# Latents ahead of the context between two layers, and three heads summed in PSUM at the end

## The chip, the cores and the metric

The kernel runs on one NeuronCore of a Trainium2 chip. The metric is the device time of one execution in microseconds (us). Before the change the median of three runs was 1581.88 us (1580.87 to 1582.18).

## What is computed

A two-layer backbone on 512 latent tokens and 256 context tokens of width 1024, all in fp32. Cut to what matters here:

```python
for i in range(2):
    shift, scale, gate = split(silu(c) @ ada_w[i] + ada_b[i])        # and the same from c_ctx
    h  = rms(x,   norm_g[i]) * (1 + scale)   + shift                 # latents
    hc = rms(ctx, norm_g[i]) * (1 + scale_c) + shift_c               # context
    yc, y = hgrn2_mixer(hc, h, ...) if i == 0 else rglru_mixer(hc, h, ...)
    x = x + gate * y
    if i == 0:
        ctx = ctx + gate_c * yc
return rms(x, final_norm_g)
```

Layer 0 (HGRN2) has 16 heads, each with four input projections, a recurrence and an output projection `w_out`. Layer 1 (RG-LRU) has 8 heads of 256 channels. Each takes `h @ w_in` (a branch `xb` for latents and context, a gate branch `g` for latents alone), a convolution over four tokens, sigmoid gates `r` and `i` by two 256x256 products in two directions, `a = exp(-8 r softplus)`, `u = sqrt(1 - a^2) * i * xb`, a linear scan in both directions, `(forward + backward) * silu(g)`, and an output product with its 256 rows of `w_out`. Layer 1 needs the context only to start its latent scans.

## The kernel before, in words

All tensors lie with channels on the 128 partitions and the 768 tokens (context in columns 0 to 255, latents in 256 to 767) along the free axis. The residual stream `x1` is 8 tiles of 128 channels. A product in fp32 precision is made of three float32r matmuls (`mm3`, L307): high times high, high times low, low times high. So every weight, loaded as 512 KB of raw fp32 by the SP queue, is split by ScalarE (`hi`, L129) and VectorE (`lo`, L130). The split weights have three buffers each (`hip`, `lop`), the raw ones three (`rawp`); `W.slots` lets named weights use other buffers. `Weights.get` takes the weights in the order in which the program asks for them, loads three ahead, and splits the next one early while `presplit` is set.

PSUM has eight banks, four in the pool `dps` (`dtile`) and four in `aps` (`atile`). The tile framework orders each engine's instructions from the program's order, its own estimate of what is ready, and priorities (`high_priority(n)` lifts an instruction by n places); each engine then runs its list strictly in order. `issue_after` keeps ScalarE's table sets together.

**Between the layers.** The program runs head 15's recurrence (L720) with the sum of the outputs of heads 12 to 14 as filler. A block of the adaLN product (`ada_block`, L224: 16 matmuls in fp32 on raw weights, a copy, 4 small matmuls) is woven into each of heads 9 to 14 by `extra` (L707); the last block of layer 1, number 5, goes into head 14. Then come: the output of head 15 (`out_item` with `accs`, L391), first for the 256 context tokens, all eight channel tiles, then for the 512 latents. After each tile VectorE adds gate times PSUM to `x1` (L405), ScalarE squares it (L285, L288) and GpSimd (tiles 1 to 3) or VectorE (tiles 5, 6) adds the square to one of three accumulators (L289). `norm1` makes the reciprocal root mean square of each segment: matmuls against a column of ones (L262), a square root (L265), a reciprocal (L266), a broadcast by matmuls (L272). Then `hchunk` (L296) normalizes one channel tile (VectorE L300, ScalarE L304, VectorE L305), and the first products of layer 1, into four `dtile` banks and one `atile` bank, follow tile by tile: first all context tiles (`rc`, two banks), then all latent tiles (`rl`, three banks; L739 to L743). `conv` (L776) evacuates them with a priority of 400. `rin(0, ALL[1:2])` (L895) is the product that follows.

**Layer 1.** For each head j a `mixer` (L817) first makes the gates: for each of four keys (direction, channel half) four PSUM tiles and sigmoids (L840). Then follow tanh and two exponentials per key (L849 to L852), square roots (L858), and the scans (L863 to L867), with the sum, the silu gate and the split of y (`yh` L872, `yl` L873). `phase` weaves other products in between: those of the next head (`rin`) and the output of the head before (`rout`, L881), whose eight PSUM tiles VectorE adds to `x1` (L879). R, Gt and T have four buffers each, y two. Heads 0 to 5 take `rin` of the next head whole. Head 6 takes only its `xb` part with its gates, and `rout(5)` behind them. The last head takes its own `g` part while three of its four keys' gates are made, and the fourth key as a group of its own. Then come `rout(6)`, the last head's output for its first channel half (`part(d, (0,), ...)`), where tiles 5 to 7 are added at once and tiles 0 to 4 stay in PSUM, and for its second half in two column halves, each with adds, squares, sums and the final norm (L937 to L956).

## Time and profile before

| | us |
|---|---|
| median of 3 runs | 1581.88 |
| the profiled execution, its own time | 1581.96 |
| its span, first to last instruction | 1580.2 |
| TensorE busy in the span | 1531.5 |
| VectorE, ScalarE, GpSimd busy | 1207.8, 902.6, 12.7 |

The mean granted TensorE clock is 0.985 of full speed. Times in the trace count from the start of the span. In a row of the timeline the first figure is the start, the second the length; in brackets stands how long the engine had been idle before, and what ended it. A matmul's length includes its way through the array, so a run of them is counted from start to start. L is a line of the kernel. Layer 0 ends, and layer 1 starts, around 1075 to 1133 us; the last head of layer 1 begins at about 1502.

### The profile page before, as it was taken

Reading aid. Unit: us, or ns where it says so; the run is one execution under the profiler, and the core shown is the slowest. Engines: PE = TensorE matmul, PEld = TensorE weight load, DVE = VectorE, ACT = ScalarE, POOL = GpSimd, SP = SyncE. Lnnn points to the kernel's source line nnn. Section 1 sums busy time; section 2 is a strip of 40 time slices with the busy share of each in tenths; the row PEclk is TensorE's granted clock in tenths of the full one; section 3 lists DMA queues with packets and bytes.
Section 4 is the critical chain, followed back from the end, with each engine's and each line's share of the span. In section 5 each row is a group of like instructions: output and inputs, shape, how many; then the busy total and the mean of one; then the engine's idle time right before and its main releaser. Section 6 shows DMA issues by size and latency. Waiting matters only on the chain.

```text
span 1580.2 us, 34022 instructions
## 1 busy us (share of the span) xinstructions
PE 1531.5 (97%) x14740; PEld 1431.9 (91%) x14740; DVE 1207.8 (76%) x1867; ACT 902.6 (57%) x1423; POOL 12.7 (1%) x16
## 2 busy tenths in 40 slices
PE   5999999999999999999999999998999999999995
PEld 3899999999999999999999999987889988988984
DVE  4767678768867868867876786787768887797888
ACT  4554555555554554554545555654577577667874
POOL 0000000000000000000000000001000000000001
PEclk8999999999999999999999999998999999999996
DMA  8231311110211211223232132202212213222111
GB/s 324 84 121 55 95 55 41 55 55 28 82 41 42 68 41 55 81 68 95 68 95 82 55 108 68 95 15 67 67 54 81 83 51 94 80 77 70 55 53 54
DMA packets 33861, 116.80 MB, mean 74 GB/s; under 512 B 3632, under 2 KB 6064, under 8 KB 33712
## 3 DMA queue, kind: packets, MB, share of 16 engines
q1 hardware_dynamic: 32192, 113.26, 23.0%
q8 instruction: 116, 1.90, 0.5%
q10 hardware_dynamic: 1520, 1.37, 0.3%
q14 instruction: 33, 0.27, 0.1%
HBM read 112.52 MB, written 2.10 MB: 73 GB/s over the span
## 4 chain that ended last, share of the span: by engine, by line
PE 93%; DVE 3%; ACT 2%; issue 1%; POOL 1%; DMA 0%; POOLq 0%; ACTq 0%; DVEq 0%
PE in L311 12%; PE in L312 11%; PE in L313 11%; PE v L381 9%; PE lv L460 4%; PE r L313 4%; PE r L312 4%; PE r L311 4%; PE o L565 4%; PE gt L311 3%; PE gt L312 3%; PE gt L313 3%; PE o L311 3%; PE o L313 3%; PE o L312 3%; PE U L533 2%
## 5 line engine op out<-in xcount | busy, mean ns | idle before, releaser
L311 PE MATMUL in<-h_hi,hi 128*128 128x384 f32 x1024 | 350.6, 343 | 3.4 <-ACT h_hi L304 2.7
L312 PE MATMUL in<-h_lo,hi 128*128 128x384 f32 x1024 | 345.8, 338 | 0.3 <-DVE h_lo L305 0.3
L313 PE MATMUL in<-h_hi,lo 128*128 128x384 f32 x1024 | 344.9, 337 | 0.0
L130 DVE TENSOR_TENSOR lo<-raw,hi 128x1024 fp32r<-128x1024 f32 x160 | 195.2, 1220 | 88.1 <-ACT hi L129 84.7
L129 ACT ACTIVATE hi<-raw 128x1024 fp32r<-128x1024 f32 x160 | 168.2, 1057 | 121.3 <-PE in L312 48.7
L311 PEld LDWEIGHTS in<-h_hi,hi 128*128 128x128 f32 x1024 | 193.1, 189 | 16.8 <-issue 9.9
L312 PEld LDWEIGHTS in<-h_lo,hi 128*128 128x128 f32 x1024 | 193.1, 189 | 2.8 <-issue 1.6
L313 PEld LDWEIGHTS in<-h_hi,lo 128*128 128x128 f32 x1024 | 192.8, 189 | 1.2 <-issue 0.8
L509 DVE TENSOR_TENSOR QQ<-QQ,T 128x768 f32<-128x768 f32 x112 | 117.8, 1052 | 20.8 <-ACT qt L491 20.5
L416 ACT ACTIVATE kt<-KK 128x768 f32<-128x768 f32 x112 | 102.4, 915 | 41.1 <-DVE KK L502 32.7
L502 DVE TENSOR_TENSOR KK<-KK,T 128x768 f32<-128x768 f32 x112 | 117.6, 1050 | 9.7 <-ACT kt L416 8.2
L313 PE MATMUL r<-h_hi,lo 128*128 128x512 f32 (+1 forms) x344 | 123.4, 359 | 0.3 <-DVE lo L130 0.3
L312 PE MATMUL r<-h_lo,hi 128*128 128x512 f32 (+1 forms) x344 | 123.1, 358 | 0.0
L311 PE MATMUL r<-h_hi,hi 128*128 128x512 f32 (+1 forms) x344 | 122.9, 357 | 0.0
L337 ACT ACTIVATE sg<-in 128x384 f32<-128x384 f32 x128 | 61.5, 482 | 99.9 <-PE in L313 99.7
L381 PE MATMUL v<-hi,h_hi 128*128 128x256 f32 x384 | 111.3, 290 | 0.0
L381 PE MATMUL v<-hi,h_lo 128*128 128x256 f32 x384 | 107.4, 280 | 0.0
L381 PE MATMUL v<-lo,h_hi 128*128 128x256 f32 x384 | 107.3, 279 | 0.0
L588 DVE RECIPROCAL sq<-sq 128x384 f32<-128x384 f32 x30 | 76.3, 2545 | 21.1 <-ACT sq L582 20.9
L405 DVE SCALAR_TENSOR_TENSOR x<-o,ada,x 128x256 f32<-128x256 f32 (+1 forms) x184 | 82.3, 488 | 11.3 <-PE o L313 10.6
L311 PE MATMUL o<-rhi,hi 128*128 128x384 f32 (+2 forms) x240 | 85.0, 356 | 1.5 <-DVE lo L130 1.2
L313 PE MATMUL gt<-xh,lo 128*128 128x384 f32 x256 | 86.0, 336 | 0.0
(207 smaller groups left out, 3284.4 us busy)
## 6 DMA issues: line engine op xcount, KB each, us to landing
raw<-in_hgw_dram SPq DMA_DIRECT2D x64, 512.0 KB, 3.7
raw<-in_ada_dram SPq DMA_DIRECT2D x48, 512.0 KB, 4.2
raw<-in_rgi_dram SPq DMA_DIRECT2D x32, 512.0 KB, 3.6
raw<-in_hgv_dram SPq DMA_DIRECT2D x16, 512.0 KB, 3.6
raw<-in_hgo_dram SPq DMA_DIRECT2D x16, 512.0 KB, 3.6
raw<-in_rgg_dram SPq DMA_DIRECT2D x16, 512.0 KB, 3.6
raw<-in_rgo_dram SPq DMA_DIRECT2D x16, 512.0 KB, 3.6
x<-in_x_dram SPq DMA_DIRECT2D x8, 384.0 KB, 5.9
```

What stands on the lines that cost most here:

```text
L129: self.nc.scalar.activation(hi, r, AF.Copy)
L130: self.nc.vector.tensor_tensor(lo, r, hi.bitcast(F32), ALU.subtract)
L311: PE.matmul(ps, lhsT=wh, rhs=xh, start=first and i == 0, stop=False, skip_group_check=skip)
L312: PE.matmul(ps, lhsT=wh, rhs=xl, start=False, stop=False, skip_group_check=skip)
L313: PE.matmul(ps, lhsT=wl, rhs=xh, start=False, stop=last and i == n - 1, skip_group_check=skip)
L381: PE.matmul(ps, lhsT=xh[:, kk, t], rhs=w[:, k], start=part == 0 and k == 0 and i == 0 and c % 2 == 0, stop=part == 1 and k == 3 and i == 2 ...
L405: V.scalar_tensor_tensor(xs, ps[:, a - c.start:b - c.start], gate[:, d, 1 - j:2 - j], xs, ALU.mult, ALU.add)
L416: A.activation(view(kt, 0, [[2 * B, n], [B, 2], [1, B]]), view(KK, 0, [[2 * B, n], [NT + B, 2], [1, B]]), AF.Copy)
L460: PE.matmul(ps[w * g:w * g + w, w * c:w * c + w], lhsT=kt[:, o:o + w], rhs=rhs, start=c == 0, stop=c == NC - 1, skip_group_check=True, til ...
L502: V.tensor_tensor(kv, kv, view(T, 1, [[2, n], [m - 1, 2], [0, B]]), ALU.mult)
L509: V.tensor_tensor(qv, qv, view(T, m + 1, [[2, n], [-m - 1, 2], [0, B]]), ALU.mult)
L588: V.reciprocal(rs, rs)
```

## The change

Between the layers the adaLN block 5 moves from head 14 to the place behind the latents of head 15's output; the latents' output, norm, chunks and first products go ahead of those of the context, the context's output tiles stand one by one behind the latents' chunks, and its norm and products come last. Block 5's raw weights and the split weight of the first `g` product get wide buffers of layer 0. `conv` of head 0 has no priority any more. At the end, head 6 takes the rest of `rin(7)`; the outputs of heads 5, 6 and 7 are summed in the eight PSUM banks (`held`) and added to `x1` once; the last head's four keys are one group; and the final tiles go in the order 4 to 7, 0 to 3, with the groups of the sum of squares to match.

```diff
--- before.py
+++ after.py
@@ -288,7 +288,7 @@
             A.activation(t, x1[:, k, c], AF.Square)
             (nc.gpsimd if i == 0 and len(groups) == 3 else V).tensor_tensor(accs[i][:, c], accs[i][:, c], t, ALU.add)
 
-    THREE = ((0, 1, 2, 3), (4, 5, 6), (7,))
+    THREE, LAST = ((0, 1, 2, 3), (4, 5, 6), (7,)), ((4, 5, 6, 7), (0, 1, 2), (3,))
 
     segs = (slice(0, CTX), slice(CTX, NT))
     lat = segs[1]
@@ -388,14 +388,12 @@
                         A.activation(st[2 * g + u]["V"][:, 2 * b:2 * b + 2], src[:, :, P * u:P * u + P], AF.Copy)
                 yield 1300.0
 
-    def out_item(heads, accs=None, done=None):
+    def out_item(heads):
         ws = [wget("out", h) for h in heads]
         gate = ada[0][:, 2]
-        parts = segs if accs else halves
-        order = [(d, i) for d in range(DK) for i in range(2)]
-        for d, i in sorted(order, key=lambda x: x[1]) if accs else order:
+        for d, i in [(d, i) for d in range(DK) for i in range(2)]:
             e = slice(P * d, P * d + P)
-            c = parts[i]
+            c = halves[i]
             ps = dtile(f"o{heads[0]}_{d}_{i}")[:, :c.stop - c.start]
             mm3(ps, [(w[0][:, e], w[1][:, e], st[h]["r"][0][:, c], st[h]["r"][1][:, c]) for h, w in zip(heads, ws)])
             for j, g in enumerate(segs):
@@ -404,10 +402,6 @@
                     xs = x1[:, d, a:b]
                     V.scalar_tensor_tensor(xs, ps[:, a - c.start:b - c.start], gate[:, d, 1 - j:2 - j], xs,
                                            ALU.mult, ALU.add)
-            if accs:
-                sumsq(accs, THREE, lambda n: ktp.tile([P, NT], F32, name=n, tag="kt"), d, c)
-                if d == DK - 1:
-                    done(i)
             yield 490.0 * len(heads)
 
     def gather(KK, kt, B):
@@ -611,6 +605,9 @@
     for i in range(16):
         W.slots["ada", 0, i // 4, i % 4] = (rawp, "raw", 1024) if i in (10, 11) else wide[(i if i < 10 else i - 2) % 6]
     W.slots["v", 0, 0] = (wide[2], wide[0])
+    for j in range(4):
+        W.slots["ada", 1, 5, j] = wide[(0, 1, 5, 1)[j]]
+    W.slots["rin", 0, 1, 0] = (wide[0], wide[1])
 
 
     acc0 = kdp.tile([P, NT], F32, name="acc0", tag="kd")
@@ -707,7 +704,7 @@
     def extra(h):
         if h in (1, 2):
             return [ada_block(0, 3 + h)]
-        return [ada_block(1, h - 10)] if h >= 10 else []
+        return [ada_block(1, h - 10)] if 10 <= h < NH - 1 else []
 
     for h in range(NH):
         if h == 0:
@@ -721,26 +718,46 @@
         run_all(side)
     accs1 = [pl.tile([P, n], F32, name=f"acc1_{i}", tag=t)[:, :NT]
              for i, (pl, t, n) in enumerate(((kdp, "kd", NT), (qp, "q", NT), (sp, "S", 2 * (NC - 1) * P)))]
-    rs1 = []
-
-    def norm1(i):
+    rs1 = {}
+
+    def norm1(i, between=()):
         c = segs[i]
-        rs1.extend(rstd_of([chunks(a, c) for a in accs1], ones_d, f"h1_{i}", ((c.stop - c.start) // P,)))
-
-    run_all(out_item((NH - 1,), accs1, norm1))
+        rs1[i], = rstd_of([chunks(a, c) for a in accs1], ones_d, f"h1_{i}", ((c.stop - c.start) // P,), between)
+
+
+
+    w15 = wget("out", NH - 1)
+
+    def out_last(d, i):
+        e, c = slice(P * d, P * d + P), segs[i]
+        ps = dtile(f"o{NH - 1}_{d}_{i}")[:, :c.stop - c.start]
+        mm3(ps, [(w15[0][:, e], w15[1][:, e], st[NH - 1]["r"][0][:, c], st[NH - 1]["r"][1][:, c])])
+        V.scalar_tensor_tensor(x1[:, d, c], ps, ada[0][:, 2, d, 1 - i:2 - i], x1[:, d, c], ALU.mult, ALU.add)
+        sumsq(accs1, THREE, lambda n: ktp.tile([P, NT], F32, name=n, tag="kt"), d, c)
+
+    for d in range(DK):
+        out_last(d, 1)
+    side = ada_block(1, 5)
+    for _ in range(4):
+        next(side)
+    norm1(1, side)
 
 
     W.presplit = False
     wx = [wget("rin", 0, 0, e) for e in range(2)]
-    first = [[(w, dtile(f"rc{e}")[:, :CTX]) for e, w in enumerate(wx)]]
     wg = wget("rin", 0, 1, 0)
-    first.append([(w, (dtile if e < 2 else atile)(f"rl{e}")) for e, w in enumerate(wx + [wg])])
-    scr = [ktp.tile([P, NT], F32, name=f"scr1_{k}", tag="kt") for k in range(2)]
-    for i, c in enumerate(segs):
+    first = {1: [(w, (dtile if e < 2 else atile)(f"rl{e}")) for e, w in enumerate(wx + [wg])]}
+    for i in (1, 0):
+        c = segs[i]
         for k in range(DK):
-            hchunk(1, k, i, rs1[i], scr[k % 2])
+            hchunk(1, k, i, rs1[i], ktp.tile([P, NT], F32, name=f"scr1_{i}_{k}", tag="kt"))
             for w, ps in first[i]:
                 mm3(ps, hpairs(w, c, [k]), first=k == 0, last=k == DK - 1)
+            if i:
+                out_last(k, 0)
+        if i:
+            norm1(0)
+            first[0] = [(w, dtile(f"rc{e}")[:, :CTX]) for e, w in enumerate(wx)]
     W.presplit = True
     l0.close()
 
@@ -773,7 +790,7 @@
             turn["gsig"] = A.activation(s["gs"][:, e], ps, AF.Sigmoid)
         V.tensor_tensor(s["gs"][:, e], ps, s["gs"][:, e], ALU.mult)
 
-    def conv(j, e, i, ps):
+    def conv(j, e, i, ps, last=1):
 
         s = rt[j]
         if "xb" not in s:
@@ -785,12 +802,13 @@
         n = segs[i].stop - segs[i].start
         cw = prm_("conv_w").rearrange("p (c t) -> p c t", t=4)[:, 2 * j + e]
         urgent = ExitStack()
-        urgent.enter_context(tc.high_priority(400))
+        if j:
+            urgent.enter_context(tc.high_priority(400))
         A.activation(y, ps, AF.Identity, scale=cw[:, 2:3], bias=prm_("conv_b", 2 * j + e, 1))
         for tap, sh in ((1, 1), (0, 2), (3, -1)):
             src, dst = (ps[:, :n - sh], y[:, sh:]) if sh > 0 else (ps[:, 1:], y[:, :n - 1])
             V.scalar_tensor_tensor(dst, src, cw[:, tap:tap + 1], dst, ALU.mult, ALU.add)
-        if i == 1:
+        if i == last:
             A.activation(s["xh"][:, e], xb, AF.Copy)
             V.tensor_tensor(s["xl"][:, e], xb, s["xh"][:, e].bitcast(F32), ALU.subtract)
         urgent.close()
@@ -818,8 +836,6 @@
 
 
         s = rt[j]
-        yh = s["yh"] = yp.tile([P, 2, LAT], F32R, name=f"yh{j}", tag="yh")
-        yl = s["yl"] = yp.tile([P, 2, LAT], F32R, name=f"yl{j}", tag="yl")
         comb, parts = {}, {}
         for keys in groups:
             for d, jc in keys:
@@ -841,6 +857,9 @@
                     yield 1.0
                 V.tensor_tensor(Gt, Gt, s["xb"][:, jc], ALU.mult)
             yield None
+            if "yh" not in s:
+                s["yh"], s["yl"] = [yp.tile([P, 2, LAT], F32R, name=f"{t}{j}", tag=t) for t in ("yh", "yl")]
+            yh, yl = s["yh"], s["yl"]
 
             for d, jc in keys:
                 R, Gt, T = comb[d, jc]
@@ -888,43 +907,47 @@
             add_out(ps, d, early)
             yield 1300.0
 
-    for i in range(2):
+    for i in (1, 0):
         for e in range(2):
-            conv(0, e, i, first[i][e][1])
+            conv(0, e, i, first[i][e][1], 0)
     g_evac(0, 0, first[1][2][1])
     run_all(rin(0, ALL[1:2]))
+    def part(ws, j, d, us, c):
+        e = slice(P * d, P * d + P)
+        return [(ws[u][0][:, e], ws[u][1][:, e], rt[j]["yh"][:, u, c], rt[j]["yl"][:, u, c]) for u in us]
+
+
+    pss = []
+
+    def held(j, ds, ws):
+        ws.extend([] if ws else [wget("rout", 2 * j + e) for e in range(2)])
+        for d in ds:
+            if len(pss) == d:
+                pss.append((dtile if d < 4 else atile)(f"ro{d}"))
+            mm3(pss[d], part(ws, j, d, (0, 1), slice(0, LAT)), first=j == RH - 3, last=False, skip=True)
+            yield 1300.0
+
     for j in range(RH):
-        last = j == RH - 1
-        m = mixer(j, (((0, 0), (1, 0), (0, 1)), ((1, 1),)) if last else (((0, 0), (1, 0), (0, 1), (1, 1)),))
+        m = mixer(j, (((0, 0), (1, 0), (0, 1), (1, 1)),))
         if j < RH - 2:
             phase(m, 8.0, rin(j + 1, ALL[:2]), 10400.0)
             phase(m, 20.0, chain_([rin(j + 1, ALL[2:])] + ([rout(j - 1)] if j else [])), 26000.0 if j else 15600.0)
-        elif not last:
+        elif j < RH - 1:
             phase(m, 8.0, rin(j + 1, ALL[2:]), 5000.0)
-            phase(m, 20.0, rout(j - 1), 10400.0)
+            for _ in range(4):
+                next(m)
+            phase(m, 12.0, rin(j + 1, ALL[:2]), 5200.0)
         else:
-            phase(m, 6.0, rin(j, ALL[:2]), 10400.0)
-            run_all(m)
-
-
-    run_all(rout(RH - 2, 0))
-    j = RH - 1
-    s = rt[j]
+            w5 = []
+            phase(m, 8.0, held(j - 2, range(4), w5), 5200.0)
+            run_all(held(j - 2, range(4, DK), w5))
+            phase(m, 20.0, held(j - 1, range(DK), []), 10400.0)
+
+
     accs2 = [cp.tile([P, NT], F32, name=f"acc2{i}", tag="R") for i in range(3)]
     ws = [wget("rout", 2 * j + e) for e in range(2)]
-
-    def part(d, us, c):
-        e = slice(P * d, P * d + P)
-        return [(ws[u][0][:, e], ws[u][1][:, e], s["yh"][:, u, c], s["yl"][:, u, c]) for u in us]
-
-    pss = []
     for d in range(DK):
-        ps = (dtile if d < 4 else atile)(f"ro{j}_{d}")
-        mm3(ps, part(d, (0,), slice(0, LAT)), last=d >= 5, skip=True)
-        if d < 5:
-            pss.append(ps)
-        else:
-            add_out(ps, d, 0)
+        mm3(pss[d], part(ws, j, d, (0,), slice(0, LAT)), first=False, last=False, skip=True)
     H, rsf = LAT // 2, []
     fin = [[pl.tile([P, 2, NT], F32, name=f"fin{i}_{t}", tag=t)[:].rearrange("p u n -> p (u n)")[:, :4 * H]
             .rearrange("p (k n) -> p k n", k=4) for pl, t in o] for i, o in
@@ -937,12 +960,12 @@
     for i in range(2):
         c = slice(H * i, H * i + H)
         cx = slice(CTX + H * i, CTX + H * i + H)
-        for d in range(DK):
-            ps = pss[d][:, c] if d < 5 else (dtile if i else atile)(f"ro{j}_{d}_{i}")[:, :H]
-            mm3(ps, part(d, (1,), c), first=d >= 5, last=d >= 5 or i == 1, skip=True)
+        for n, d in enumerate((4, 5, 6, 7, 0, 1, 2, 3)):
+            ps = pss[d][:, c]
+            mm3(ps, part(ws, j, d, (1,), c), first=False, last=i == 1, skip=True)
             add_out(ps, d, 0, cx)
-            sumsq(accs2, THREE, lambda n: cp.tile([P, NT], F32, name=n, tag="G"), d, cx)
-            if i == 1 and d == 4:
+            sumsq(accs2, LAST, lambda n: cp.tile([P, NT], F32, name=n, tag="G"), d, cx)
+            if i == 1 and n == 4:
                 stats(0)
     stats(1)
     for i, rs in enumerate(rsf):
```

## Rows read from the trace of the kernel before

**Rows 1.** The page: TensorE's busy time, and the chain that ended last.

```profile
PE 1531.5 (97%) x14740; PEld 1431.9 (91%) x14740; DVE 1207.8 (76%) x1867; ACT 902.6 (57%) x1423; POOL 12.7 (1%) x16
...
PE 93%; DVE 3%; ACT 2%; issue 1%; POOL 1%; DMA 0%; POOLq 0%; ACTq 0%; DVEq 0%
```

**Rows 2.** Busy time by stretch; columns: PE, PEld, DVE, ACT, POOL, clock, DMA share, GB/s.

```profile
1030.00:1045.00 15.00, 11.92 (x287) 10.23 (x287) 14.95 (x24) 8.59 (x12) 0.00 (x0) 1.00 0.11 37
1075.40:1078.20 2.80, 0.81 (x5) 0.41 (x3) 2.70 (x4) 2.80 (x5) 0.00 (x0) 0.95 0.21 25
1078.20:1081.60 3.40, 3.35 (x15) 3.15 (x16) 3.40 (x6) 1.59 (x4) 0.47 (x1) 0.54 0.79 280
...
1091.40:1094.80 3.40, 0.11 (x2) 0.02 (x1) 3.30 (x4) 2.51 (x4) 3.25 (x2) 1.00 0.07 11
1094.80:1105.30 10.50, 10.50 (x50) 10.50 (x51) 6.97 (x15) 3.17 (x7) 0.00 (x0) 0.51 0.29 96
...
1075.40:1133.40 58.00, 50.24 (x243) 42.45 (x242) 47.12 (x78) 31.87 (x53) 7.75 (x6) 0.88 0.21 64
```

**Rows 3.** TensorE's timeline between the layers.

```profile
1075.25 0.34 PE L313 MATMUL o<-r,lo 128*128 128x384 f32 x1
...
1094.78 1.68 PE L262 MATMUL msh<-cst,acc 128*128 128x1 f32 x8 [3.29 <-POOL acc L289]
...
1128.47 0.40 PE L311 MATMUL r<-h_hi,hi 128*128 128x512 f32 x1
...
1133.14 0.40 PE L313 MATMUL r<-h_hi,lo 128*128 128x512 f32 x1
```

**Rows 4.** GpSimd's timeline between the layers.

```profile
1089.80 4.92 POOL L289 TENSOR_TENSOR acc<-acc,sq 128x512 f32<-128x512 f32 x3 [5.53 <-ACT sq L288]
```

**Rows 5.** VectorE's timeline between the layers.

```profile
1109.73 1.41 DVE L300 SCALAR_TENSOR_TENSOR scr<-x,amul,rbh 128x512 f32<-128x512 f32 x2
1111.98 2.50 DVE L792 SCALAR_TENSOR_TENSOR xb<-rc,prm,xb 128x255 f32<-128x255 f32 x6 [0.85 <-ACT xb L789]
```

**Rows 6.** TensorE by line and form, whole span: all twelve adaLN blocks.

```profile
L230 PE MATMUL ada<-raw,sc 128*32 128x256 f32 x384 | 32.5, 412 | 14.0 <-DMA raw<-in_ada_dram 14.0
...
L240 PE MATMUL adat<-cst,blk 128*128 128x2 f32 x96 | 11.5, 241 | 0.7 <-ACT blk L236 0.7
```

**Rows 7.** Busy time by stretch, as rows 2, last head.

```profile
1541.00:1548.20 7.20, 0.00 (x0) 0.00 (x0) 7.20 (x8) 5.80 (x9) 0.00 (x0) 0.82 0.00 0
1548.20:1555.80 7.60, 7.27 (x15) 4.91 (x16) 7.46 (x11) 2.90 (x3) 0.00 (x0) 0.50 0.00 0
```

**Rows 8.** TensorE's timeline at the end.

```profile
1548.20 2.09 PE L311 MATMUL ro<-yh,hi 128*128 128x512 f32 x3 [7.53 <-ACT yh L872]
...
1557.91 0.99 PE L311 MATMUL ro<-yh,hi 128*128 128x256 f32 x7
```

**Rows 9.** VectorE by line, 1485 to 1580 us: busy, mean ns, idle before.

```profile
L879 DVE SCALAR_TENSOR_TENSOR x<-ro,ada,x 128x512 f32<-128x512 f32 (+1 forms) x35 | 20.6, 623 | 2.7 <-PE ro L313 2.7
...
L861 DVE TENSOR_TENSOR G<-G,T 128x768 f32<-128x768 f32 x8 | 7.4, 948 | 0.0
L863 DVE TENSOR_TENSOR_SCAN T<-R,G 128x768 f32<-128x768 f32 x4 | 7.0, 1748 | 0.0
...
L867 DVE TENSOR_TENSOR_SCAN T<-R,T,G 128x512 f32<-128x512 f32 x4 | 5.1, 1280 | 0.0
...
L871 DVE TENSOR_TENSOR T<-T,gg 128x512 f32<-128x512 f32 x4 | 2.7, 684 | 0.0
```

**Rows 10.** ScalarE's timeline in the last head.

```profile
1525.63 0.58 ACT L840 ACTIVATE G<-gt,prm 128x384 f32<-128x384 f32 x1 [0.25 <-PE gt L313]
...
1535.22 1.28 ACT L858 ACT_TABLE_LOAD   x1
1536.51 2.32 ACT L858 ACTIVATE T<-T 128x768 f32<-128x768 f32 x3
...
1547.52 0.63 ACT L872 ACTIVATE yh<-T 128x512 fp32r<-128x512 f32 x1 [1.38 <-DVE T L871]
```

## The prediction

> **What bounds the kernel now.** First the page: TensorE is busy for 97% of the span, and 93% of the chain that ended last is TensorE's [rows 1]. So elsewhere only fewer or shorter matmuls would help, and the change removes none. What it can win is time in which TensorE stands still or runs at half clock (1.2 instead of 2.4 GHz). Next the busy time by stretch. It shows two such places, and the change touches both.
>
> Between the layers, from the last matmul for heads 12 to 14 to the first gates of layer 1 (1075.4 to 1133.4), TensorE is busy for 50.24 of 58.0 us at a mean clock of 0.88 [rows 2]. That is 7.8 us idle and 58.0 x 0.12 = 7.0 us lost to the clock. At full clock the work is 43.2 us. Two gaps stand out: 2.0 of 2.8 us idle while head 15's result and weight are split, with 3.4 us near half clock behind it, and 3.3 us for the latents' sum of squares, with 10.5 us at half clock behind that [rows 2]. The timeline names GpSimd's accumulator as what ended the second [rows 3]; three adds took it 4.92 us [rows 4].
>
> In the last head TensorE stands for 7.53 us until the first half of y is there [rows 8], and then runs 7.6 us at half clock, while VectorE is busy throughout [rows 7]. Here VectorE and ScalarE set the end.
>
> The sum is made against the profiled execution: 1581.96 us, a span of 1580.2 and 1.8 around it; the median of the runs, 1581.88, is the same within 0.1. A difference under 0.2% (3.2 us) counts as none.
>
> **Prices.** A matmul of 512 columns costs 0.2335 us from start to start (20 steps from 1128.47 to 1133.14 [rows 3]). I scale by columns: 0.117 for 256, 0.175 for 384. A matmul of the sum of squares costs 0.21 at half clock (8 in 1.68 [rows 3]), so 0.105 at full. An adaLN block is 32.5 / 12 + 11.5 / 12 = 2.7 + 1.0 us of TensorE [rows 6].
>
> **Part 1, block 5 moves.** It leaves head 14, and 3.7 us of TensorE with it. The start of the next head is bound by VectorE (14.95 of 15 us, TensorE 11.92 [rows 2]), so not all of this need come through. Ends: 0 and 3.7. I take 2.8, three quarters, since TensorE had to deliver that head's projections before VectorE could start. The four loads move on the SP queue too, ahead of the first `rin` weights. The last needs the buffer of head 14's result, free at the last matmul for heads 12 to 14, 1075.25 [rows 3]. SP issues in order, so three `rin` weights queue behind it. They are wanted only behind the latents' norm some 15 us later, so I take nothing; if the cover fails, each waiting load delays the latents' products directly.
>
> **Part 2, latents first.** The work becomes 43.2 + 3.7 = 46.9 us. The losses, place by place:
> - Start. The split of the same weight and result is awaited, so the loss stays: 2.0 idle and half of 3.4 for the clock, 3.7 us.
> - The latents' sum. GpSimd's adds end as late as before against the last output tile, 3.3 us. Now the block's 2.7 us and the context's output tiles (24 x 0.117 = 2.8 us) can stand there. Behind the sum come root, reciprocal, broadcast and the first chunk. VectorE's step is 0.7 (two in 1.41 [rows 5]) and ScalarE's similar; the block's 1.0 us of small matmuls hides the reciprocal. I take 1.5 us idle and no loss of clock. Ends: 0, if context tiles fill it, and the old 3.3 + 5.25.
> - The latents' products. 72 x 0.2335 = 16.8 us; a tile takes TensorE 2.1 us with its context tile another 0.35, VectorE two steps of 0.7 and an add of 0.42, as long as a step of `conv` on 256 columns (six in 2.50 [rows 5]). VectorE keeps up. The `conv` that held up a chunk for 1.2 us is gone from here.
> - The context's sum and chunks, now last. Behind the last output tile stand add, square, sum, root, reciprocal, broadcast and two chunk steps: some 4.2 us, of which TensorE works 1.1. What should fill it is the product `rin(0,1,1)` (24 x 0.2335 = 5.6 us). It needs one of the four `dtile` banks: two hold the latents' products until `conv` has read them, two are the context's. Its weight also needs head 15's buffer. So I take the 3.1 us as idle and 1.7 for the clock, 4.8 in all. Then the context's products go at VectorE's pace (two steps of 0.42, 0.84 a tile, against 0.70 on TensorE) with `rin(0,1,1)` beside them, and this outlasts the `conv` and split before head 0's gates.
>
> Sum: 46.9 + 3.7 + 1.5 + 4.8 = 56.9 against 58.0, so 1.1 won here and 2.8 in head 14: **3.9 us**. Ends: 46.9 + 3.7 alone gives 7.4 + 3.7 = 11.1 won; the slower rival below gives 8 lost.
>
> **Part 3, heads 5 to 7 in PSUM.** 19 adds of 512 columns (8 for head 5, 8 for head 6, 3 early ones of head 7) leave VectorE; the row has 35 with 16 of 256 columns [rows 9]. TensorE's work is the same, only in another order: `rin(7)` first, then gates with half of `held(5)`, its other half and `held(6)`. Busy throughout, it reaches the end of `held(6)` at the old 1540.7 (1548.20 less 7.53 [rows 8]). Behind the last gate lie 24 + 48 matmuls, 16.8 us, so the gates end at 1523.9. Head 6's scans must have freed R and G by then; they lose 8 adds ahead of them (0.6 each, as the adds of 512 columns in L871 less their overlap), so I see no stall. ScalarE: last sigmoid 0.6, then 12 activations of 0.87 (nine and a table load between 1526.1 and 1535.22 [rows 10]), two weight splits of 1.0, two table loads of 1.28, one root of 0.8 (three in 2.32): 1540.3. VectorE, each less its 0.08 of overlap [rows 9]: product 0.87, scan 1.67, product 0.87, scan 0.6 and 1.2, sum and gate 0.6 each: 6.4, so 1546.7, and the split 0.5: 1547.2 against 1548.20 [rows 8]. The merged group costs three more activations before the roots; the adds gone and the third scan no longer in between pay for it. TensorE restarts at half clock after 6.5 us idle; I take the same 7.6 us [rows 7], so 24 matmuls last 9.0 us and end at 1556.2. The second half of y follows 7.0 us of VectorE behind the first and is ready at 1554.9. So the last products start at 1556.2 instead of 1557.91 [rows 8]: 1.7 us. The tail is bound by VectorE and loses one add and one split of 0.6: 1.2 us. Regrouping the squares I cost at nothing, as GpSimd's group is still first. **2.9 us** in all; ends -2 (the y of the first half held up by a third scan, 2.5 us) and +5 (full clock).
>
> ScalarE loaded a table in 1.28 us and began the next root 0.01 us later [rows 10]. The Trainium skill ("ScalarE: Activation LUTs", What ACT_TABLE_LOAD costs) states 2.66 us for a switch, with a drain in it. By the page the two switches in the chain would make it 2.8 us longer and the forecast 1577.8; the row shows no drain, and I go by the row.
>
> **Sum.** 1581.96 - 3.9 - 2.9 = 1575.2, rounded to **1575.0 us**.
>
> **Rivals.**
> (a) *The gaps fill.* The planner puts context tiles and the next product into every hole and the clock stays up: 11.1 + 5 won, 1566. For: it did interleave both segments' products. Against: the banks above.
> (b) *Only one place pays.* The context path at the end gives back what the latents won, or the merged group holds up the first half of y: 3 won, 1579, or nothing, 1582.
> (c) *Slower: two bare norm chains at half clock.* Before, the latents' output hid the context's norm. If context tiles don't fill the first chain and nothing fills the second, each drops the clock as the one before did for 10.5 us [rows 2]: 1.5 + 5.25 for the first; for the second 3.1 idle, 24 + 24 half-speed products 5.6 longer, and some 3.8 until weight and bank for `rin(0,1,1)` are there. Then 46.9 + 3.7 + 6.75 + 12.5 = 69.9, 11.9 lost, 2.8 and 2.9 won: 1588. It decides from 6.8 us above the losses that I count. For: sparse matmuls did leave the clock low. Against: 5.5 us of ready work for the first chain. The Trainium skill ("TensorE: Matmul & The Clock Gate", Why this matters for your kernels) also warns of idle gaps between bursts; the trace agrees, with a fall after 3.3 us and one after 2.0.
> (d) *The change doesn't do what it says*: the planner had the order already. Unlikely; the rows show context first.
>
> **Chances.** The forecast 0.50, (a) 0.20, (b) 0.17, (c) 0.10, (d) 0.03. Range: (a) and most of (b), 1566 to 1581.5. Faster by over 0.2% (under 1578.8): forecast, (a) and a third of (b), 0.76; within it 0.13; slower 0.11.
>
> **What would show it.** Right: no gap on GpSimd's accumulator before the latents' sum, block 5 there, clock 1.0 over the latents' products; the loss between the layers at 10 us; 16 adds at L879's place instead of 35, first half of y at about 1547 less 3.9. Wrong: half clock through the context's products, gates of head 7 waiting for R or G, or TensorE idle for over 7.5 us in the last head.

## The result, and the profile of the changed kernel

The changed kernel takes **1599.47 us** (median of four runs, 1599.44 to 1599.61), the kernel before beside it 1581.38. The ratio is 1.0116, with a 95% interval from 1.0103 to 1.0129. I had forecast 1575.0: wrong in sign, and outside the range. The profiled execution took 1599.44, with a span of 1597.7. Starts on TensorE place the loss:

| event | before | after | later by |
|---|---|---|---|
| transposes of head 14 | 1004.86 | 1006.59 | 1.73 |
| gates of head 0 in layer 1 | 1133.37 | 1149.30 | 15.93 |
| first half of y in the last head | 1548.20 | 1568.22 | 20.02 |
| last products (256 columns) | 1557.91 | 1576.33 | 18.42 |
| end of the span | 1580.2 | 1597.7 | 17.5 |

So 1.7 us come from head 14 and 14.2 from the stretch between the layers. The recurrent heads give 0.7 back (from mixer 1 on the traces run 15.27 apart), and the end adds 2.2. The page, against [rows 1]:

```profile
PE 1537.7 (96%) x14740; PEld 1435.3 (90%) x14740; DVE 1195.2 (75%) x1848; ACT 898.4 (56%) x1420; POOL 11.4 (1%) x16
...
PE 90%; DVE 4%; ACT 4%; issue 1%; DMA 0%; POOL 0%; POOLq 0%; ACTq 0%; DVEq 0%
```

TensorE has as many matmuls as before, VectorE 19 instructions fewer, as counted. But TensorE is busy for 6.2 us more, so more of it ran at half clock, and 3% of the chain went to VectorE and ScalarE. Busy time between the layers by stretch, against [rows 2] (same columns):

```profile
1076.80:1149.30 72.50, 59.68 (x285) 47.72 (x284) 49.34 (x82) 32.58 (x55) 6.46 (x6) 0.84 0.21 66
1076.80:1079.30 2.50, 1.74 (x26) 0.68 (x24) 2.28 (x3) 2.50 (x5) 0.00 (x0) 1.00 0.46 105
...
1088.60:1103.90 15.30, 9.24 (x41) 8.78 (x41) 5.81 (x10) 3.82 (x9) 2.53 (x2) 0.60 0.12 35
1103.90:1110.00 6.10, 6.10 (x19) 4.99 (x20) 3.08 (x4) 1.94 (x3) 0.00 (x0) 0.61 0.26 86
...
1125.40:1132.00 6.60, 5.15 (x25) 4.08 (x24) 4.45 (x8) 3.96 (x7) 0.00 (x0) 0.78 0.25 79
1132.00:1134.60 2.60, 0.87 (x5) 0.68 (x3) 1.77 (x5) 2.47 (x5) 0.00 (x0) 0.89 0.00 0
1134.60:1143.60 9.00, 8.17 (x51) 7.87 (x52) 8.58 (x19) 3.35 (x8) 0.00 (x0) 0.81 0.00 0
```

Before, 58.0 us held 7.8 idle and 7.0 lost to the clock; now 72.5 hold 12.8 (72.50 less 59.68) and 11.6 (72.5 x 0.16). Nearly all of it stands in two places: around the latents' norm (6.1 idle in 1088.60:1103.90, clock 0.60) and around the context's, from 1125.40 on. TensorE's timeline, against [rows 3]:

```profile
1091.56 0.58 PE L262 MATMUL msh<-cst,acc 128*128 128x1 f32 x2 [3.32 <-POOL acc L289]
...
1093.28 1.85 PE L240 MATMUL adat<-cst,blk 128*128 128x2 f32 x8
1095.99 2.29 PE L262 MATMUL msh<-cst,acc 128*128 128x1 f32 x10 [0.86 <-DVE acc L289]
...
1100.13 2.07 PE L272 MATMUL rbh<-cst,rh 128*128 128x128 f32 x8 [0.57 <-DVE rh L266]
...
1103.87 0.80 PE L311 MATMUL rl<-h_hi,hi 128*128 128x512 f32 x1 [1.66 <-ACT h_hi L304]
...
1127.45 0.72 PE L262 MATMUL msh<-cst,acc 128*128 128x1 f32 x5 [1.45 <-DVE acc L289]
...
1134.60 0.50 PE L311 MATMUL rc<-h_hi,hi 128*128 128x256 f32 x2 [1.73 <-ACT h_hi L304]
...
1149.30 0.52 PE L311 MATMUL gt<-xh,hi 128*128 128x384 f32 x2
```

The 3.3 us on GpSimd's accumulator are there as before, and behind them nothing but one-column sums, block 5's small matmuls and the broadcast until the latents' products at 1103.87: no context tile stands in between. The context's chain has nothing beside it either. VectorE at the second accumulate of the latents' squares, and ScalarE at the last two of these squares:

```profile
1095.16 0.16 DVE L245 TENSOR_TENSOR ada<-adat,prm 128x4 f32<-128x4 f32 x1 [3.11 <-PE adat L240]
1095.24 0.69 DVE L289 TENSOR_TENSOR acc<-acc,sq 128x512 f32<-128x512 f32 x1
...
1089.69 1.14 ACT L288 ACTIVATE sq<-x 128x512 f32<-128x512 f32 x2
```

The accumulate stood behind block 5's addition, which waited 3.11 us for `adat`, though the squares had been there since 1090.83. The Trainium skill ("PSUM — Partial Sum Buffer", Engine vs sequencer instructions) says that VectorE's queue is a strict FIFO; the row agrees.

At the end, TensorE against [rows 8], ScalarE against [rows 10], VectorE against [rows 9]:

```profile
1568.22 0.80 PE L311 MATMUL ro<-yh,hi 128*128 128x512 f32 x1 [12.07 <-ACT yh L891]
```

```profile
1544.88 1.99 ACT L129 ACTIVATE hi<-raw 128x1024 fp32r<-128x1024 f32 x2
...
1553.65 1.28 ACT L877 ACT_TABLE_LOAD   x1
1554.94 0.85 ACT L877 ACTIVATE T<-T 128x768 f32<-128x768 f32 x1
```

```profile
L898 DVE SCALAR_TENSOR_TENSOR x<-ro,ada,x 128x256 f32<-128x256 f32 x16 | 6.6, 474 | 4.9 <-PE ro L313 4.9
...
1555.82 0.96 DVE L880 TENSOR_TENSOR G<-G,T 128x768 f32<-128x768 f32 x1 [2.16 <-ACT T L877]
1556.77 1.23 DVE L130 TENSOR_TENSOR lo<-raw,hi 128x1024 fp32r<-128x1024 f32 x1
1557.91 1.75 DVE L882 TENSOR_TENSOR_SCAN T<-R,G 128x768 f32<-128x768 f32 x1
1559.58 1.80 DVE L880 TENSOR_TENSOR G<-G,T 128x768 f32<-128x768 f32 x2
1561.29 0.68 DVE L885 TENSOR_TENSOR_SCAN T<-R,G 128x256 f32<-128x256 f32 x1
1561.89 1.73 DVE L882 TENSOR_TENSOR_SCAN T<-R,G 128x768 f32<-128x768 f32 x1
...
1564.72 0.93 DVE L880 TENSOR_TENSOR G<-G,T 128x768 f32<-128x768 f32 x1
...
1566.17 0.69 DVE L885 TENSOR_TENSOR_SCAN T<-R,G 128x256 f32<-128x256 f32 x1
1566.77 0.67 DVE L890 TENSOR_TENSOR T<-T,gg 128x512 f32<-128x512 f32 x1
```

The 19 additions are gone (16 at L898 instead of 35), yet TensorE waits 12.07 us instead of 7.53. Before the first half's gate product (1566.77) VectorE does four steps for the second half: two products (one of the two at 1559.58, and 1564.72) and two scans (1561.89, 1566.17). A weight split (1556.77) stands in between as well.

### The profile page after: what moved, and what is told of

Read it like the earlier page. It is cut to its first block, busy times and chain, and to the rows that moved or that the text cites. A ratio compares the mean times of both kernels' runs of the same rounds, so it can differ in the third digit from the quotient of the medians.

```text
span 1597.7 us, 33997 instructions
## 1 busy us (share of the span) xinstructions
PE 1537.7 (96%) x14740; PEld 1435.3 (90%) x14740; DVE 1195.2 (75%) x1848; ACT 898.4 (56%) x1420; POOL 11.4 (1%) x16
## 4 chain that ended last, share of the span: by engine, by line
PE 90%; DVE 4%; ACT 4%; issue 1%; DMA 0%; POOL 0%; POOLq 0%; ACTq 0%; DVEq 0%
PE in L311 11%; PE in L312 11%; PE in L313 11%; PE v L381 9%; PE r L313 4%; PE r L312 4%; PE r L311 4%; PE lv L454 4%; PE o L559 4%; PE gt L311 3%; PE gt L312 3%; PE gt L313 3%; PE o L311 3%; PE o L312 3%; PE o L313 3%; PE U L527 2%
## 5 line engine op out<-in xcount | busy, mean ns | idle before, releaser
L129 ACT ACTIVATE hi<-raw 128x1024 fp32r<-128x1024 f32 x160 | 168.0, 1057 | 123.9 <-PE in L312 51.3
L312 PE MATMUL gt<-xl,hi 128*128 128x384 f32 x256 | 85.8, 335 | 0.0
```

Source lines behind the costliest of these rows:

```text
L129: self.nc.scalar.activation(hi, r, AF.Copy)
L312: PE.matmul(ps, lhsT=wh, rhs=xl, start=False, stop=False, skip_group_check=skip)
```

## The experiments

One table for all. "Gates" is the start of head 0's gates in layer 1 (before: 1133.37), "stretch" the time to it from the last matmul for heads 12 to 14 (before: 58.1), "rest" the time from it to the end of the span (before: 446.8), "median" that of the runs. The first three come from one profiled execution each. They scatter where nothing was changed, too: that last matmul starts between 1074.3 and 1075.9 (after: 1076.8), the old stretch takes 58.1 to 58.9 us (before, e2, e8, e10, e13), and the old end 445.5 to 446.8.

| kernel | gates | stretch | rest | median | ratio to before (95%) |
|---|---|---|---|---|---|
| after | 1149.30 | 72.5 | 448.4 | 1599.47 | 1.0116 (1.0103, 1.0129) |
| e1_between_only | 1147.66 | 72.5 | 445.5 | 1594.50 | 1.0084 (1.0069, 1.0099) |
| e2_end_only | 1133.31 | 58.9 | 449.0 | 1584.17 | 1.0022 (1.0012, 1.0031) |
| e9_after_again | 1147.67 | 72.5 | 448.2 | 1597.35 | 1.0099 (1.0084, 1.0114) |
| e3_block5_in_head14 | 1144.58 | 69.7 | 448.3 | 1594.43 | 1.0082 (1.0067, 1.0097) |
| e4_block5_sum_late | 1145.14 | 70.3 | 447.3 | 1593.91 | 1.0078 (1.0063, 1.0093) |
| e5_cover_first | 1137.00 | 61.9 | 448.2 | 1588.21 | 1.0049 (1.0034, 1.0064) |
| e6_cover_second | 1141.99 | 66.8 | 447.1 | 1590.65 | 1.0062 (1.0047, 1.0077) |
| e7_cover_both_old_end | 1133.11 | 58.0 | 446.0 | 1581.33 | 1.0002 (0.9992, 1.0011) |
| e11_warm | 1129.93 | 55.2 | 446.4 | 1578.92 | 0.9979 (0.9969, 0.9990) |
| e12_root_first | 1130.94 | 55.1 | 446.3 | 1579.77 | 0.9992 (0.9983, 1.0002) |
| e14_root_first_warm | 1126.35 | 51.8 | 446.2 | 1575.37 | 0.9962 (0.9950, 0.9975) |
| e16_before_warm | 1128.88 | 54.6 | 446.1 | 1578.36 | 0.9984 (0.9976, 0.9993) |
| e8_one_group | 1133.23 | 58.1 | 454.7 | 1589.70 | 1.0059 (1.0044, 1.0074) |
| e10_half_held | 1133.53 | 58.9 | 449.8 | 1584.62 | 1.0025 (1.0016, 1.0035) |
| e13_y_first | 1132.78 | 58.3 | 444.8 | 1579.40 | 0.9991 (0.9982, 1.0000) |
| e15_e14_e13 | 1126.40 | 51.3 | 445.6 | 1573.75 | 0.9953 (0.9941, 0.9965) |

**The two places apart** (e1, e2, e9). The first has the end of before, the second the end of after alone; the third is after once more.

```diff
-        m = mixer(j, (((0, 0), (1, 0), (0, 1), (1, 1)),))
+        m = mixer(j, (((0, 0), (1, 0), (0, 1)), ((1, 1),)) if last else (((0, 0), (1, 0), (0, 1), (1, 1)),))
...
-            phase(m, 20.0, held(j - 1, range(DK), []), 10400.0)
+            phase(m, 6.0, rin(j, ALL[:2]), 10400.0)
+            run_all(m)
```

> The kernel of after with the end of before (two groups of gates for the last head, products of head 6 added to x one by one, old order of the last sums); the order between the layers and block 5 as in after. Theory 1: the two places don't touch each other, so what was read by shifting the traces adds up: the gates of head 0 start at about 1149.3 us instead of 1133.4, mixer 1 stands 15.3 us late, and the time is 1581.4 + 15.3 = 1596.7 us. Rival 2: the late start is partly hidden by the slack in the recurrent heads when the old end follows, or the end is what costs: under 1590 us.

> The kernel before with the end of after alone (sums of heads 5 to 7 held in PSUM, one group of gates, new order of the last sums); head 14 and the stretch between the layers as before. Theory 1: the end by itself loses 2.2 us, since its first half of y is ready 4.7 us later (ScalarE works through four heads' tanh, two exp and two weight splits in one row) and 2.5 us come back after it: 1583.6 us, TensorE idle 12 us ahead of the last products. Rival 2: the loss of 2.2 us is carried in by the shifted stretch before it, and the end by itself gives the 2.9 us that the prediction worked out: 1578.5 us.

> The kernel of after once more, nothing changed. In its first profile the granted clock fell to 0.50 beside head 14 at 1004 us behind 1.33 us of idle time; two kernels with the same instructions up to there had the same idle time and a clock of 1.00, and stood 1.7 us better at the end of that head. Theory 1: whether the clock falls there differs from kernel to kernel or from run to run at the same instructions: here the end of that head's transposes may lie at either place, and the time at 1597.5 to 1599.5 us. Rival 2: after falls every time, 1599.5 us with the clock at 0.50 again.

They add up: +13.5 and +3.1 us against before, where after has +18.1 and, repeated, +16.4. e1 is 2.2 us below its forecast: the 1.7 us of head 14 didn't come again. After, e1 and e9 issue the same instructions up to there and have the same idle time; the clock fell in the first profile alone. TensorE's timeline and a stretch, of after and then of e1:

```profile
1000.90 0.61 PE L454 MATMUL lv<-qt,kt 128*32 128x32 f32 x46 [1.33 <-ACT qt L485]
...
1004.00:1006.00 2.00, 2.00 (x8) 2.00 (x7) 0.00 (x0) 0.00 (x0) 0.00 (x0) 0.50 0.00 0
```

```profile
1000.87 0.61 PE L454 MATMUL lv<-qt,kt 128*32 128x32 f32 x46 [1.34 <-ACT qt L485]
...
1004.00:1006.00 2.00, 2.00 (x17) 1.97 (x16) 0.00 (x0) 0.98 (x1) 0.00 (x0) 1.00 0.00 0
```

Before, with block 5's matmuls beside the scores, head 14's projections still ran at that time, and the clock stayed up. So the change opened a gap of 1.3 us that cost 1.7 us in one profile and nothing in three (e1, e4, e9). What decides between the two is not shown: each is one profiled execution. Nor is it shown that the spread of e9's runs (1596.32 to 1599.31) comes from this gap.

**Block 5** (e3, e4). In e3 it goes back beside head 14's scores; in e4 its sum goes behind the whole stretch.

```diff
-        return [ada_block(1, h - 10)] if 10 <= h < NH - 1 else []
+        return [ada_block(1, h - 10)] if h >= 10 else []
```

> The kernel of after with adaLN's block 5 back beside the scores of head 14; all else as in after. Theory 1: head 14 gets back what it lost, the last matmul of the outputs of heads 12 to 14 comes 1.5 us earlier, the granted clock around 1004 us is 1.00 again, and in the gap the accumulate of the latents' squares no longer stands behind the block's addition on VectorE (some 2 us): 1596 us. Rival 2: head 14's loss is a mere shift of 1.5 us that has nothing to do with block 5, and the gap gets emptier and slower without it: 1599 to 1602 us.

```diff
-    norm1(1, side)
+    norm1(1)
...
+    run_all(side)
     W.presplit = True
```

> The kernel of after, but the second half of block 5 (the products that gather its sums, and the two additions on VectorE) comes behind the whole stretch instead of ahead of the latents' broadcast. Theory 1: VectorE stood 3.1 us at that addition with the second accumulate of the latents' squares queued behind it; without it the first matmul of the latents' products comes some 2 to 3 us earlier, and the time is about 1597 us. Rival 2: the accumulate on POOL ends the wait all the same, TensorE only idles longer: 1599.5 us.

Against e1 and e9 (1147.7) the gates come 3.1 us earlier with the block in head 14 and 2.5 earlier with its sum behind the loop; 0.3 of each lies ahead of the stretch, which is 2.8 and 2.2 us shorter. The wait in VectorE's queue is thus worth about 2.2 us: e4's first latents' product starts at 1099.79 instead of 1101.98 in e1. In head 14 the block costs nothing that shows: the transposes start at 1004.50 in e3 and 1004.86 before, with it, and without it at 1004.62 to 1004.99 in e4, e9 and e1. Both kernels came out faster than forecast (1594.43 for 1596, 1593.91 for 1597).

**The two bare norm chains** (e5, e6, e7; all with block 5 in head 14, e7 with the old end).

```diff
     for d in range(DK):
         out_last(d, 1)
+    for d in range(DK):
+        out_last(d, 0)
...
-            if i:
-                out_last(k, 0)
```

> The kernel of after with block 5 back in head 14 and with the context's eight output tiles moved from the loop of the latents' products to the place right behind the latents' output tiles, where the latents' sum of squares is awaited. Theory 1: TensorE's 5 us of context tiles fill the latents' bare norm chain, the clock stays up over the latents' products, and the idle time that the loop had at its end (a chunk behind context additions on VectorE) is gone: 6 to 8 us better than the kernel with block 5 back (1594.4), so 1587 us. Rival 2: the additions and squares of the context's tiles go ahead of the latents' root and chunks on VectorE and ScalarE, and the chain gets longer by what is filled: 1593 to 1596 us. Rival 3: the second bare chain, the context's, costs most of the loss: no more than 3 us better.

```diff
-            if i:
-                out_last(k, 0)
+            if i and k < 4:
+                out_last(2 * k, 0)
+                out_last(2 * k + 1, 0)
+            if i and k == 5:
+                norm1(0)
```

> The kernel of after with block 5 back in head 14; in the loop of the latents' products two context tiles go with each of the first four chunks, and the context's sum, root and broadcast go behind the sixth chunk instead of behind the loop. Theory 1: the context's products follow the latents' without the 1.5 + 3.0 us of idle time and the half clock behind them: 5 to 6 us better than the kernel with block 5 back (1594.4), so 1589 us; the latents' chain ahead of the loop stays bare. Rival 2: the context's additions on VectorE, now two a chunk, hold up the latents' chunks and TensorE waits in the loop instead: 1592 to 1595 us.

e7 takes the first edit, and `norm1(0)` behind chunk 3.

> Block 5 in head 14 and the end as in the kernel before; between the layers the latents go first as in the change, but the context's output tiles stand ahead of the latents' broadcast and the context's sum, root and broadcast within the loop of the latents' products, so that neither norm chain is bare. Theory 1: the losses of the change between the layers are those of the two bare chains; with both filled, what remains are 3.7 us at the start and some 2 us in the two chains, the gates of head 0 start at about 1129 us instead of 1133.4, and the time is 1577 us, under that of the kernel before. Rival 2: the order itself (latents ahead of the context) is what costs, by split, sum on GpSimd and bank conflicts: 1585 us or more.

With block 5 in head 14 the gates stand 11.2 us late (1144.58). Covering the first chain gives 7.6 of it back, covering the second 2.6, both together 11.5; the stretch is shorter by 7.8, 2.9 and 11.7. So what the stretch grew by (58.1 to 72.5) is the two bare chains, 11.7, and 2.8 for the block. e5 came near its forecast of 1587, e6 between its two. But e7, forecast at 1577, only drew level. Its stretches around the latents' norm and products:

```profile
1087.80:1099.80 12.00, 9.69 (x51) 9.10 (x51) 7.71 (x16) 5.18 (x13) 2.19 (x3) 0.58 0.10 24
1099.80:1109.00 9.20, 9.20 (x32) 7.86 (x33) 6.95 (x13) 4.34 (x7) 0.00 (x0) 0.62 0.06 25
```

TensorE is busy for 18.9 of 21.2 us there, and the clock is low all the same.

**The clock** (e11, e12, e14, e16). e11, e14 and e16 compute matmuls whose result nothing reads. e11 is e7 with them. e12 is e7 with the latents' reciprocal ahead of the last three context additions, and the latents' squares summed in two accumulators instead of three. e14 is e12 with such matmuls, and e16 is before with them, its order unchanged.

```diff
+    def warm(n, name):
+        ps = dtile(name)
+        for i in range(n):
+            PE.matmul(ps, lhsT=w15[0][:, :P], rhs=st[NH - 1]["r"][0][:, lat], start=i == 0, stop=i == n - 1)
     for d in range(DK):
         out_last(d, 1)
+    with tc.high_priority(300):
+        warm(5, "wa")
...
     norm1(1)
+    warm(8, "wb")
```

> The kernel with both chains covered and the old end (1581.3), with 13 matmuls of 512 columns more that nothing reads: five behind the latents' last output tile, eight behind the products that sum their squares, ahead of the broadcast. Theory 1: with both chains covered, what is left of the loss is the clock, at 0.58 and 0.62 for 21 us though TensorE was busy for 19 of them; a clock that stays up gives back some 8 us, less 3.0 for the matmuls added where TensorE had work: 1574 to 1577 us. Rival 2: the clock falls all the same at the one-column products of the sum, and the added matmuls cost their 3 to 6 us: 1583 to 1587 us.

```diff
-    for d in range(DK):
+    for d in range(5):
         out_last(d, 0)
-    norm1(1)
+    norm1(1, (out_last(d, 0) for d in range(5, DK)))
...
-        sumsq(accs1, THREE, lambda n: ktp.tile([P, NT], F32, name=n, tag="kt"), d, c)
+        sumsq(accs1, TWO if i else THREE, lambda n: ktp.tile([P, NT], F32, name=n, tag="kt"), d, c)
```

> The kernel with both chains covered and the old end (1581.3), with the latents' reciprocal ahead of the last three context tiles in VectorE's order, and the latents' squares summed in two accumulators instead of three. Theory 1: the reciprocal stood 2.3 us behind three additions of context tiles, and four of twelve one-column products of the sum (eight of the trace's records, 0.21 us each at half clock, 1.7 us) leave the chain: the latents' products start 3 to 4 us earlier, 1578 us. Rival 2: the start of the products is earlier, but the clock stays low as long: 1580 to 1581 us.

> The kernel with both chains covered, the reciprocal ahead of the last context tiles and two accumulators (1579.8), with 17 matmuls of 512 columns more that nothing reads, five behind the latents' last output tile and twelve around the broadcast. Theory 1: in that kernel TensorE stood for 1.6 and 3.4 us in the latents' chain and the clock was 0.70 for 9.2 us of the products behind it; with these gaps filled it stays up and the products lose 2.8 us less: 1577 us. Rival 2: the added matmuls delay the sum or the broadcast by as much as the clock gives: 1579 to 1581 us.

```diff
                 if d == DK - 1:
+                    if i:
+                        ps = dtile("wa")
+                        for n in range(14):
+                            PE.matmul(ps, lhsT=ws[0][0][:, :P], rhs=st[NH - 1]["r"][0][:, lat], start=n == 0, stop=n == 13)
                     done(i)
```

> The kernel before, context first as it was, with 14 matmuls of 512 columns more that nothing reads in the gap of 3.29 us ahead of the latents' sum. Theory 1: what can be won between the layers is the clock, whatever goes first: behind that gap it was at 0.51 for 10.5 us, and with the gap filled the 5.2 us lost there come back in the larger part: 1576 to 1578 us, as good as the kernel with the latents first and matmuls added (1578.9). Rival 2: the clock falls behind the gap all the same, because of the one-column products of the sum, or the products are held by VectorE anyway: 1580 to 1582 us.

e11 came out 2 us above the first theory's range and 4 below the second's. e12 lies between its two: the latents' products started 2.1 us earlier (1097.68 instead of 1099.76; 2.8 earlier counted from the start of the stretch), not 3 to 4, and the clock was low behind it, as the second had it. e14 is 1.6 us better than expected, and e16 0.4 above what the first theory gave. First the same two stretches in e11, in e12 and in e14, then two stretches of [rows 2] in e16:

```profile
1087.80:1099.80 12.00, 10.53 (x52) 9.39 (x52) 8.07 (x16) 5.32 (x13) 2.25 (x4) 0.72 0.14 44
1099.80:1109.00 9.20, 8.90 (x45) 7.50 (x46) 9.20 (x16) 6.01 (x10) 0.00 (x0) 1.00 0.01 2
```

```profile
1087.80:1099.80 12.00, 7.43 (x52) 6.94 (x53) 10.94 (x22) 7.08 (x16) 3.25 (x4) 0.95 0.14 44
1099.80:1109.00 9.20, 9.20 (x32) 7.55 (x33) 7.56 (x13) 5.08 (x8) 0.00 (x0) 0.70 0.00 0
```

```profile
1087.80:1099.80 12.00, 11.63 (x67) 9.70 (x66) 11.11 (x23) 7.44 (x17) 2.48 (x3) 1.00 0.00 0
1099.80:1109.00 9.20, 9.20 (x49) 7.80 (x49) 8.32 (x13) 3.29 (x6) 0.00 (x0) 1.00 0.21 61
```

```profile
1091.40:1094.80 3.40, 3.40 (x21) 2.90 (x20) 3.40 (x6) 2.39 (x5) 1.30 (x1) 1.00 0.00 0
1094.80:1105.30 10.50, 9.91 (x72) 9.12 (x72) 10.29 (x21) 6.23 (x12) 0.00 (x0) 1.00 0.32 101
```

With the gaps filled the clock is 1.00 in e14 and e16. e14's gates come 4.6 us earlier than e12's, and e16's 4.5 earlier than before's; 1.3 and 0.9 of that lie ahead of the stretch, so in the stretch of these profiles the added matmuls were worth 3.3 and 3.5 us. By the medians, each against before beside it, they won 4.7 us over e12 and 2.9 over before. e16's single times spread from 1576.63 to 1581.72, and the profiled one, 1576.77, is among the fastest. In the old order, too, what could be won between the layers was the clock.

**The end** (e8, e10, e13). e8 is before with one group of gates (and the pace of `phase` that goes with it); e10 is before with sums of heads 5 and 6 held for four of eight tiles, and the gates in two groups; e13 is e2 with VectorE's work for the second half of y behind the first.

```diff
-        m = mixer(j, (((0, 0), (1, 0), (0, 1)), ((1, 1),)) if last else (((0, 0), (1, 0), (0, 1), (1, 1)),))
+        m = mixer(j, (((0, 0), (1, 0), (0, 1), (1, 1)),))
...
-            phase(m, 6.0, rin(j, ALL[:2]), 10400.0)
+            phase(m, 8.0, rin(j, ALL[:2]), 10400.0)
```

> The kernel before with one change: the four gates of the last head in one group instead of three and one; sums, stretch between the layers and head 14 as before. Theory 1: the one group is what costs at the end: the first half of y waits for 12 activations in a row instead of 9 and a third scan on VectorE, TensorE idles some 11 to 12 us ahead of the last products instead of 7.5, and the time is 1583 to 1584 us. Rival 2: the group costs nothing, as a table load and a wait are saved, and what the end of the change lost came from the products held in PSUM (weight splits among the activations): 1581 us.

```diff
-            phase(m, 6.0, rin(j, ALL[:2]), 10400.0)
+            phase(m, 6.0, half_held(j - 2, 400), 10400.0)
             run_all(m)
...
-    run_all(rout(RH - 2, 0))
+    run_all(half_held(RH - 2, 0))
```

> The kernel before with only the sums held in PSUM, and the last head's gates still in two groups (three and one): the first four of eight output tiles of heads 5 and 6 stay in PSUM and take head 7's products, the other four are added to x as before; head 7's projections of x go ahead of head 5's products. Theory 1: the sums are the good part of the end and the one group is its bad part: eight additions of 512 columns leave VectorE, half of them from the stretch in which the first half of y is made, the first half of y comes 1 to 3 us earlier than at 1548.2 us, and the time is 1578 to 1580 us. Rival 2: VectorE's additions only filled its waits, the scans and ScalarE set the end: 1581 us. Rival 3: the bank that four held tiles take from dtile delays head 7's gates: 1583 us.

```diff
             for d, jc in keys:
                 R, Gt, T = comb[d, jc]
+                held_back = after("y0") if j == RH - 1 and jc == 1 else ExitStack()
...
-                    V.tensor_tensor(y, y, s["gs"][:, jc], ALU.mult)
+                    gated = V.tensor_tensor(y, y, s["gs"][:, jc], ALU.mult)
+                    if jc == 0:
+                        turn["y0"] = gated
```

> The kernel before with the end of after alone (1584.2), and in its last head VectorE's work for the second half of y held behind the gate product of the first half, so that no third scan stands in it. Theory 1: the step that failed at the end is that order: the scan of the second half (1.7 us) and two of its products (0.9 each) stood ahead of the first half of y. It is then ready about 3.3 us earlier, the second half is ready in time all the same, and the time is 1581 us. Rival 2: the second half comes later than TensorE wants it and takes back what the first gave: 1583 to 1584 us. Rival 3: the bound is ScalarE's row of twelve activations and splits, the first half comes hardly earlier: 1584 us.

The one group alone costs 8.8 us, far more than I expected: TensorE idles 14.89 us, as the last sigmoid of the group starts at 1531.99, where the group of three had its last at 1525.63: four gates now share TensorE with head 7's projections before the first tanh. In after those projections run earlier, and the last sigmoid starts at 1539.68 less 15.27, 1524.4. Holding sums gave nothing by itself (e10, +3.7). Its two splits of head 6's output weights stand between the last gate and the first tanh, 2.00 us of ScalarE: the last sigmoid starts 0.3 us later than before (1525.95), the first tanh 2.2 later and the split of the first half of y 1.9 later. The time is near that of its third rival, but the gates hardly came later. The last products then wait another 3.61 us for the second half; why is not shown. TensorE and ScalarE's last sigmoid in e8, TensorE in e13, and ScalarE in e10:

```profile
1557.77 1.22 PE L311 MATMUL ro<-yh,hi 128*128 128x512 f32 x2 [14.89 <-ACT yh L872]
...
1531.99 0.58 ACT L840 ACTIVATE G<-gt,prm 128x384 f32<-128x384 f32 x1 [0.33 <-PE gt L313]
```

```profile
1548.89 1.22 PE L311 MATMUL ro<-yh,hi 128*128 128x512 f32 x2 [8.64 <-ACT yh L876]
```

```profile
1526.43 2.00 ACT L129 ACTIVATE hi<-raw 128x1024 fp32r<-128x1024 f32 x2
```

In e2 the first half of y is used at 1552.88, in e13 at 1548.89, 4.0 us earlier, of which 0.5 was there at the gates already: the order on VectorE was worth 3.5 us. The second half is in time, and the last products start at 1557.31 instead of 1561.29. With it the new end is better than the old by 2.0 us in the profiles (444.8 against 446.8) and by 1.8 in the medians, with an interval for the ratio that just reaches 1.0000; forecast for the end were 2.9.

**Both together** (e15).

> The two kernels before this one together: between the layers both chains covered, reciprocal first, two accumulators and 17 matmuls that nothing reads; at the end the sums in PSUM, one group of gates, the first half of y first. Theory 1: the two places add up: 1577 from the first, and the end no worse than the old one, so 1576 to 1577.5 us, under the kernel before by 0.2 to 0.3%. Rival 2: the end stays worse than the old one by 1 to 3 us: 1578 to 1580 us.

It takes 1573.75 us, a ratio of 0.9953 (0.9941 to 0.9965), better than expected, and beats before and after. The parts add up: e14 won 5.8 us and e13 1.8, and e15 wins 7.5. Most of it comes from matmuls that compute nothing: without them e12 stands at 0.9992.

## Why the prediction was wrong

Three steps failed: block 5's place in head 14, the cover of the latents' norm chain, and the order of VectorE's work for the last y. Of the signs of being wrong that it named, two came: TensorE idle for 12.07 us in the last head, and a low clock over the context's first products (0.81 in 1134.60:1143.60).

**Part 1, 2.8 us for block 5.** Wrong. The step that failed is that TensorE had to deliver head 14's projections before VectorE could start, so that three quarters of 3.7 us would come through. TensorE stood idle instead (4.20 of 6 us busy in 996 to 1002, against 5.96), and head 14's transposes came 0.1 to 0.5 us later than in e3, or 2.1 where the clock fell: nothing was won. I had bounded the term by 0 and 3.7, and not asked for the loss that a new gap brings.

**Part 2, 1.1 us between the layers.** The work was right (72.5 less the two losses is 48.1 us, forecast 46.9). Of the losses place by place:
- The start, 3.7: better than forecast in after, where block 5 filled it (1.3 idle up to 1081.60, full clock).
- The latents' sum, 1.5: this is the step that failed. It cost 14.6: 6.1 idle, 6.1 and 2.4 for the clock in the two stretches from 1088.60. I let ready context tiles "stand there". They were ready by their data, but the program gives them out in the loop, one behind each chunk, and the planner kept to that. And I used block 5's small matmuls as cover without asking what stands behind its addition in VectorE's queue; that was the 2.2 us of e4.
- The latents' products, none: about right from 1110 to 1125.40, with 0.2 us of waiting for a context addition and 0.8 for a chunk.
- The context's chain, 4.8: right in kind, and 7.5 in size (1.5 + 1.7 + 0.8 idle, 3.5 for the clock).

The losses sum to 24.4 us, where 10.0 were forecast. **Rival (c)** had the mechanism: two bare chains at half clock. That its 69.9 us for the stretch come near the measured 72.5 is in part luck: it had 6.75 for the first chain, which cost 14.6, and 12.5 for the second, which cost 7.5. I gave it 0.10, on the argument of 5.5 us of ready work. Its 1588 fell short mostly because I still credited it with the 5.7 us of parts 1 and 3. The Trainium skill's warning of idle gaps ("TensorE: Matmul & The Clock Gate", Why this matters for your kernels), which I set beside (c), spoke for it, and the trace agrees: 6.1 us idle with a clock of 0.60 in 1088.60:1103.90.

**Part 3, 2.9 us at the end.** In before's time (less 15.27) `held(6)` ended at 1540.9 (forecast 1540.7) and ScalarE's first root at 1540.5 (1540.3), weight splits in its row included. TensorE's 24 products took 8.1 us. The sum has 9.0, which its own rows don't give: 15 products in 7.6 us at half clock [rows 7] and nine more at 0.2335 make 9.7, as before. The rest took 21.4 us instead of 22.3 before (1.2 won forecast, 0.9 measured). One step failed: from the end of the root to the first product of y it took 12.4 us (1555.79 to 1568.22), not 6.9. I had written that the third scan is no longer in between. It was: the planner puts the second half's products and scans where it thinks the first half waits. I had it as an end of the range (2.5 us); it measured 3.5 in e13. The sum also put VectorE's half of a weight split at nothing, 1.23 us, which stands behind the first product in after as in e13; e13 still needs 9.0 us. The table load took 1.28 us with the next root 0.01 later, as in [rows 10]. The Trainium skill ("ScalarE: Activation LUTs", What ACT_TABLE_LOAD costs) adds a drain to a switch; these rows show none.

## What to carry to other kernels

A chain of small steps (sum, root, reciprocal, broadcast) with nothing beside it can cost its idle time and then the clock behind it. When an order is turned round, ask of each such chain what stands beside it in the order of issue, not what is ready by its data, and what the new cover holds up in the in-order queue of another engine. When a group is merged, check in which order the planner works off its members: the first one needed may come last but one. And price a half-clock stretch before any reordering: here, filling one gap in the old order (e16, 2.9 us) won more than the new order with both chains covered (e7, nothing); only the new order with its gaps filled (e14, 5.8 us) won more than that.
